# A one-core encoder layer in split fp32: layer norm by pairs of tiles, loads of the mixed rows deferred, the output weights in the common ring, head 0's operands in other memory, and two pieces of attention ordered behind feed-forward products

## The chip, the cores and the metric

The kernel runs on 1 core of one Trainium2 chip. The metric is the device time of one execution in microseconds (us), taken as the median of several runs; lower is better. The engines of the core are TensorE (PE in the profile, with its weight loads as PEld), VectorE (DVE), ScalarE (ACT), GpSimd (POOL) and SyncE (SP), which here only issues DMAs. Each engine takes its own instructions in a fixed order and waits at each for what that instruction needs.

## What is computed

One layer of a streaming encoder for 1024 new frames (the prompt) and 32 next frames of a running stream (the sample), width 1024, all in fp32. Cut to what matters:

```
mod = silu(c) @ w_ada + b_ada                      # six rows: sh1 sc1 g1 sh2 sc2 g2
h   = x * (1 + sc1) + sh1
p   = h @ w_in                                     # columns of three groups of heads
hm  = mLSTM(4 heads of p)        # matrix memory, chunk by chunk
hf  = FoX(8 heads of p)          # softmax(q k^T / 8 + F_t - F_s) v, causal
hg  = u * (tril(ws) @ layer_norm(v) + bs)          # spatial gate
mix = concat(hm, hf, hg) @ w_o
x   = layer_norm(ALPHA * x + (1 + g1) * mix, ln1_g, ln1_b)
h   = x * (1 + sc2) + sh2
y   = (silu(h @ w_gate) * (h @ w_up)) @ w_down     # inner width 2816
x   = layer_norm(ALPHA * x + (1 + g2) * y, ln2_g, ln2_b)
```

The outputs are both streams and the new state: keys, values, decays, matrix memory and its normalisers, gate values.

## The kernel before

Activations lie transposed: 128 features on the partitions, frames along the free axis, and eight such tiles (k = 0 to 7) make the width of 1024. The frames are split in group 0 (frames 0 to 511) and group 1 (512 to 1023 and the 32 of the sample). Every large product is made three times, since each operand is split in a high part that TensorE takes at full rate (float32r) and the rest: `gemm` issues hi by hi (L117), hi by lo (L118) and lo by hi (L119) for each k. So 24 matmuls make one 128-column block of an output, with 256 or 512 frames at a time. A weight block comes through `weights`: a load of 512 KB into a `raw` buffer on SP's queue (L85), a cast on ScalarE to the high part `whi` (L104), and a subtraction on VectorE to the low part `wlo` (L105). Raw buffers, high parts and low parts have three places each, the rings of the pool `wp`; a ring's place is used again when its last reader is done.

The program is emitted in the order of the code, and a scheduler then sets the order on each engine from the dependencies and its own time estimates. Code can bind it: `issue_after(x)` keeps what is emitted under it behind the instruction x.

The stages that the change touches run from about 300 to 470 us. First the input projection ends: a unit per block of columns, where `head_unit` makes head 7's queries and keys for the first 512 frames, L408 to L416, and stores what later stages need in DRAM (L89; `dqh` and `dql` are the high and low parts of all heads' queries and keys). The attention of head 7 over group 0 follows: scores (`fox_s`, L783 and L784), masked maximum (L786, L787), exponent (L792), scaling (L796, L800), transposes (`fox_t`, L819), products with the values (L827, L832). In between, ScalarE and VectorE split the mixed rows of group 0 into `tm_ah` and `tm_al` (`wo_mix`, L1007 and L1008), and projection units of the heads 2 to 4 for the second half of the frames run (`fm_unit`; the evacuation in `evac_qk` is L369 to L372 and sends keys out as `o_kT`).

Then the output projection of group 0 is made in two passes of 256 frames (`wo_range`): for each of eight blocks m a weight block, 24 matmuls, and `sublayer_end`, which on VectorE multiplies by the gate and adds the residual `wo_z` (L1074). The first block of a pass gives the pivot of the layer norm (`ln_pivot`; its ones-matmul is L932). Of the eight weight blocks six stay for the second pass. The first layer norm (`ln1`) works off a pass tile by tile, k = 0 to 7: times r (L1091), plus e (L1092), an ACTIVATE with scale and bias (L1095), a cast to the high part `tm_ah` (L1099), the subtraction for `tm_al` (L1100). The second pass is woven with the norm of the first, and the norm of the second with the projection units of the heads 5 to 7.

From about 443 us the feed-forward of group 0 runs: `up` makes a gate block and an up block per j (24 matmuls each, 256 frames at a time for j = 0, 512 from j = 1), `down` the way back. The attention over the frames 512 to 1023 (`mixers`: heads 0 to 7, chunks 4 and on of the mLSTM) is emitted ahead of it, to be taken in between its products until about 850 us. `fox` loads a head's operands from DRAM, first `qp`, then `k1` (`fox_k`), `q2`, `k2`, `v`, into tiles of the pool `mx1`. That pool lies where the pools `p1` and `sm` of the projection lay, and a load into it waits until the tiles that lay there are done. Modulation rows (`ada`, L179 to L193) are made in between too, with raw weights in the same ring.

## Time and profile before

| | |
|---|---|
| runs | 1363.7 us median of 3 (1363.5 to 1365.64) |
| profiled execution | 1364.8 us |
| its span from the first to the last instruction | 1362.7 us |
| instructions | 25189 |
| DMA packets | 120377, 221.70 MB |
| busy ACT, POOL of the span | 48%, 17% |

The profiled execution has its own time, which is 2.1 us over its span; the 2.1 us lie ahead of the first and behind the last instruction. In the timeline each row has a start and a duration in us, the engine, the line of the kernel, the operation, what it writes and reads, its shape, and in brackets how long the engine stood idle ahead of it and what ended that. Matmuls overlap: a row says 0.28 us for 128x256, but the next starts 0.12 us later.

### The profile page before, as it was taken

What the parts mean: (1) busy time and instruction counts of PE and PEld (TensorE: products, weight loads), DVE (VectorE), ACT (ScalarE), POOL (GpSimd) and SP (SyncE); (2) the same over time, 40 slices, a digit from 0 to 9 for tenths busy, and PEclk for the clock granted to TensorE, in tenths of its full rate; (3) what the DMA queues carried; (4) which work ended last, traced back from release to release, by engine and by line L of the source; (5) the groups of instructions that cost most, each with busy time, mean ns of one, the idle gap of its engine ahead of it and who ended that gap; (6) DMA issues with size and microseconds to landing.
All of it is one profiled execution on the core that took longest, in us unless ns stands there. A gap on an engine that the chain in (4) does not pass through costs nothing.

```text
span 1362.7 us, 25189 instructions
## 1 busy us (share of the span) xinstructions
PE 1327.6 (97%) x9434; PEld 1210.1 (89%) x9434; DVE 992.2 (73%) x2127; ACT 658.5 (48%) x1312; POOL 227.8 (17%) x263
## 2 busy tenths in 40 slices
PE   7999999998999899999999999999999999999996
PEld 4898988987999777888888888999999999999995
DVE  5545654678769667786776765678988988889777
ACT  3324454455436544545445354336663554545355
POOL 0202100043234200000000000373710000000341
PEclk9999999999999899999999999999999999999999
DMA  9775555546454765454344334574596758454321
GB/s 358 257 246 164 167 193 149 179 139 197 150 188 140 202 191 173 117 156 135 105 123 119 109 105 132 155 182 124 167 254 168 201 154 222 143 173 127 98 81 66
DMA packets 120377, 221.70 MB, mean 163 GB/s; under 512 B 18740, under 2 KB 64464, under 8 KB 120256
## 3 DMA queue, kind: packets, MB, share of 16 engines
q1 hardware_dynamic: 113024, 207.55, 48.7%
q0 software_dynamic: 6032, 11.94, 5.1%
q8 instruction: 74, 1.21, 0.4%
q10 hardware_dynamic: 1200, 0.62, 0.2%
q14 instruction: 47, 0.39, 0.1%
HBM read 188.13 MB, written 51.85 MB: 176 GB/s over the span
## 4 chain that ended last, share of the span: by engine, by line
PE 86%; DVE 6%; DMA 4%; ACT 2%; issue 1%; POOL 0%; SPq 0%; DVEq 0%; ACTq 0%
PE up_g L118 5%; PE up_g L119 5%; PE up_g L117 5%; PE dn_g L117 4%; PE dn_g L119 4%; PE dn_g L118 4%; PE tm_g L284 3%; PE tm_g L285 3%; PE tm_g L286 3%; PE sup_u L119 3%; PE sup_u L117 3%; PE sup_u L118 3%; PE fox_t L819 2%; PE fm_g L117 2%; PE sup_g L118 2%; PE sup_g L119 2%
## 5 line engine op out<-in xcount | busy, mean ns | idle before, releaser
L118 PE MATMUL up_g<-tm_al,up_whi 128*128 128x512 f32 (+1 forms) x384 | 141.3, 368 | 0.5 <-DVE tm_al L1100 0.5
L117 PE MATMUL up_g<-tm_ah,up_whi 128*128 128x512 f32 (+1 forms) x384 | 141.5, 370 | 0.2
L119 PE MATMUL up_g<-tm_ah,up_wlo 128*128 128x512 f32 (+1 forms) x384 | 140.6, 366 | 0.0
L1219 ACT CAST sup_whi<-sup_raw 128x1024 fp32r<-128x1024 f32 x54 | 56.0, 1048 | 90.9 <-PE dn_u L118 47.5
L117 PEld LDWEIGHTS up_g<-tm_ah,up_whi 128*128 128x128 f32 x384 | 72.8, 190 | 12.5 <-ACT tm_ah L1099 0.6
L118 PEld LDWEIGHTS up_g<-tm_al,up_whi 128*128 128x128 f32 x384 | 73.3, 191 | 11.0 <-DVE tm_al L1100 0.7
L119 PEld LDWEIGHTS up_g<-tm_ah,up_wlo 128*128 128x128 f32 x384 | 73.3, 191 | 10.7
L792 ACT ACTIVATE fox_p<-fox_s,fox_fmx 128x384 f32<-128x384 f32 (+2 forms) x96 | 55.1, 579 | 46.7 <-DVE fox_fmx L790 38.1
L104 ACT CAST up_whi<-up_raw 128x1024 fp32r<-128x1024 f32 x50 | 52.4, 1047 | 49.7 <-PE up_g L118 18.5
L1220 DVE TENSOR_TENSOR sup_wlo<-sup_raw,sup_whi 128x1024 fp32r<-128x1024 f32 x54 | 68.2, 1267 | 10.4 <-ACT sup_whi L1219 10.3
L1074 DVE SCALAR_TENSOR_TENSOR wo_z<-dn_g,start_mod,wo_z 128x512 f32<-128x512 f32 (+4 forms) x120 | 60.3, 521 | 20.1 <-PE dn_g L119 19.8
L105 DVE TENSOR_TENSOR up_wlo<-up_raw,up_whi 128x1024 fp32r<-128x1024 f32 x50 | 65.4, 1308 | 12.1 <-ACT up_whi L104 11.4
L117 PE MATMUL dn_g<-up_acth,dn_whi 128*128 128x512 f32 (+2 forms) x200 | 74.1, 371 | 0.0
L119 PE MATMUL dn_g<-up_acth,dn_wlo 128*128 128x512 f32 (+2 forms) x200 | 73.4, 367 | 0.0
L118 PE MATMUL dn_g<-up_actl,dn_whi 128*128 128x512 f32 (+2 forms) x200 | 72.9, 365 | 0.0
L824 ACT CAST fox_pth<-fox_t 128x512 fp32r<-128x512 f32 (+1 forms) x80 | 41.1, 545 | 55.9 <-PE fox_t L819 55.8
L104 ACT CAST dn_whi<-dn_raw 128x1024 fp32r<-128x1024 f32 (+1 forms) x44 | 42.7, 970 | 51.5 <-PE dn_u L118 11.2
L787 DVE TENSOR_REDUCE fox_fmx<-fox_s 128x1 f32<-128x384 f32 (+2 forms) x96 | 52.6, 552 | 13.5 <-PE fox_s L784 12.3
L825 DVE TENSOR_TENSOR fox_ptl<-fox_t,fox_pth 128x512 fp32r<-128x512 f32 (+1 forms) x80 | 49.4, 631 | 15.7 <-ACT fox_pth L824 15.5
L105 DVE TENSOR_TENSOR dn_wlo<-dn_raw,dn_whi 128x1024 fp32r<-128x1024 f32 (+1 forms) x44 | 49.5, 1126 | 12.6 <-ACT dn_whi L104 11.8
L284 PE MATMUL tm_g<-tm_whi,start_h1h 128*128 128x256 f32 (+1 forms) x192 | 55.9, 291 | 1.8 <-DVE tm_traw L355 1.7
L285 PE MATMUL tm_g<-tm_wlo,start_h1h 128*128 128x256 f32 (+1 forms) x192 | 56.1, 292 | 0.0
(663 smaller groups left out, 4788.9 us busy)
## 6 DMA issues: line engine op xcount, KB each, us to landing
up_raw<-w_gu SPq DMA_DIRECT2D x50, 512.0 KB
dn_raw<-w_dn SPq DMA_DIRECT2D x28, 512.0 KB
ada_late<-w_ada SPq DMA_DIRECT2D x24, 512.0 KB
sup_raw<-w_gu SPq DMA_DIRECT2D x20, 512.0 KB
start_dp<-w_gu SPq DMA_DIRECT2D x19, 512.0 KB
start_dp<-w_gu POOLq DMA_DIRECT2D x19, 512.0 KB, 8.0
wo_raw<-w_o SPq DMA_DIRECT2D x18, 512.0 KB
sup_raw<-start_dp SPq DMA_DIRECT2D x18, 512.0 KB
```

Source lines behind the costliest of these rows:

```text
L104: nc.scalar.copy(hi[:, :w], raw[:, :w])
L105: (eng or nc.vector).tensor_tensor(lo[:, :w], raw[:, :w], f(hi[:, :w]), ALU.subtract)
L117: nc.tensor.matmul(ps, hi, xh(k), start=start and k == 0, stop=False)
L118: nc.tensor.matmul(ps, hi, xl(k), start=False, stop=False)
L119: nc.tensor.matmul(ps, lo, xh(k), start=False, stop=stop and k == n - 1)
L284: nc.tensor.matmul(ps[:, :ncol], xh, hi, start=k == 0, stop=False)
L285: nc.tensor.matmul(ps[:, :ncol], xh, lo, start=False, stop=False)
L787: nc.vector.tensor_reduce(mxs[:, x:x + 1], s[:, :w], AX.X, ALU.max, negate=True)
L792: nc.scalar.activation(pr[:, lo:hi], banks[x][:, :hi - lo], AF.Exp, bias=mxs[:, 0:1], accum_out=sums[:, x:x + 1])
L1074: self.lastz = self.nc.vector.scalar_tensor_tensor(z[:, m, x:y], ps[:, x - a:y - a], g[i], z[:, m, x:y], ALU.mult, ALU.add)
L1219: nc.scalar.copy(h, x)
L1220: tt(l, x, f(h), ALU.subtract)
```

## The change

Five edits, all around the stages from 300 to 470 us:

1. **Pools.** The buffers of the evacuated queries and keys (`qkh`, `qkl`, `qkr`) move from the pool `sm` to a new pool `sq` between `p1` and `sm`; `wsp`, the spatial weights, moves from `p1` to `sm`. With that, the tiles of head 0 in `mx1` come to lie over other tiles.
2. **Mix loads.** The first six loads of mixed rows of group 0, with their casts and subtractions, are emitted under `issue_after` of head 7's last store of its operands.
3. **Common ring.** In the first pass of the output projection the weight blocks m = 3, 4, 5 lie in the pool `pw`, where m = 0, 1, 2 did, and these now take places of the ring in `wp`. The second pass runs over m = 2, 6, 7, 3, 4, 5, 0, 1 and loads 0 and 1 again (before: 0, 5, 6, 7, 3, 4, 1, 2, loading 3 and 4 again); the residual's second half comes in the order (2, 6), (4, 0), and the pivot is taken of the pass's first block.
4. **Norm by pairs.** For group 0 the layer norm takes two tiles per instruction on VectorE and in the cast. The ACTIVATE stays per tile, and each pair's multiplication is ordered behind the addition of the pair ahead of it.
5. **Ties.** The TensorE, ScalarE and VectorE instructions of head 0's first tile of scores are ordered behind the last matmul of the up block of j = 0, frames 256 to 511; the first two parts of mLSTM chunk 4 behind the last of the gate block of j = 1.

```diff
+    def traced(self, part):
+        n = len(self.nc.cur_bb.bb.instructions)
+        next(part)
+        return self.nc.cur_bb.bb.instructions[n:]
+    def tie(self, ins, target, engines):
+        for i in ins:
+            if i.engine in engines and "DMA" not in type(i).__name__ and "Dma" not in type(i).__name__:
+                self.tc.add_manual_dep(i, target.ins.name, ... reason="order")
...
-            hi = self.t(self.sm, [P, 272], F32R, "qkh", 2)
-            lo = self.t(self.sm, [P, 272], F32R, "qkl", 2)
-            kr = self.t(self.sm, [P, 272], F32, "qkr", 2)
+            hi = self.t(self.sq, [P, 272], F32R, "qkh", 2)
+            lo = self.t(self.sq, [P, 272], F32R, "qkl", 2)
+            kr = self.t(self.sq, [P, 272], F32, "qkr", 2)
...
-        self.store(self.dql[h, hi, :512], f(k2[lo]))
+        self.lastq = self.store(self.dql[h, hi, :512], f(k2[lo]))
...
-            w = kept.get(m) or self.weights(self.d["w_o"][m], KT, P, None, pool if m < 3 else None)
+            w = kept.get(m) or self.weights(self.d["w_o"][m], KT, P, None, pool if 3 <= m < 6 else None)
...
-                    for k in ((0, 4), (6, 2))[m // 7]:
+                    for k in ((2, 6), (4, 0))[m // 7]:
...
+        if c == 0:
+            yield from self.ln1_pairs(z, hh, hl, sl, r, e)
+            return
...
+    def ln1_pairs(self, z, hh, hl, sl, r, e):
+        nc, n = self.nc, sl.stop - sl.start
+        two = lambda x: x.unsqueeze(1).to_broadcast([P, 2, n])
+        last = None
+        for k in range(0, KT, 2):
+            yield
+            self.phase = "lna0"
+            zk = z[:, k:k + 2, sl]
+            with self.tc.issue_after(last.ins) if last else ExitStack():
+                nc.vector.tensor_tensor(zk, zk, two(r), ALU.mult)
+            last = nc.vector.tensor_tensor(zk, zk, two(e), ALU.add)
+            h = self.t(self.p2, [P, 544], F32, "sil", 2)[:, :2 * n].rearrange("p (k n) -> p k n", k=2)
+            for i in range(2):
+                nc.scalar.activation(h[:, i], zk[:, i], AF.Identity, bias=self.lnb[:, k + i, 0:1],
+                                     scale=self.lng[:, k + i, 0:1])
+            nc.scalar.copy(hh[:, k:k + 2, :n], h)
+            nc.vector.tensor_tensor(hl[:, k:k + 2, :n], h, f(hh[:, k:k + 2, :n]), ALU.subtract)
...
+                if c == 0 and (j, i) in ((0, 1), (1, 0)) and b == 512:
+                    eng = mybir.EngineType
+                    self.tie(self.tied[j], self.lastmm, (eng.PE, eng.Activation, eng.DVE))
...
+            if h == 0:
+                self.tied = [self.traced(parts[0])]
             if h in MLB:
-                parts.append(slow(self.mlstm(self.nextm)))
+                part = self.mlstm(self.nextm)
+                if h == 1:
+                    self.tied += [self.traced(part) + self.traced(part)]
+                parts.append(slow(part))
...
+        self.sq = self.pool("sq", 2, ctx=s1, side="right")
         self.sm = self.pool("sm", 2, ctx=s1, side="right")
...
-        self.wsp = self.t(self.p1, [P, 4, P], F32, "wsp")
+        self.wsp = self.t(self.sm, [P, 4, P], F32, "wsp", 1)
...
-        self.wo_mix(0, self.KORDER[0][:6])
+        with tc.issue_after(self.lastq.ins):
+            self.wo_mix(0, self.KORDER[0][:6])
...
-            del kept[3], kept[4]
-            weave(self.wo_range(st, *MM[0][1], (0, 5, 6, 7, 3, 4, 1, 2), kept, pw), self.ln1(0, st, *MM[0][0]))
+            del kept[0], kept[1]
+            weave(self.wo_range(st, *MM[0][1], (2, 6, 7, 3, 4, 5, 0, 1), kept, pw), self.ln1(0, st, *MM[0][0]))
```

How the change moves instructions is shown at three places, in the order in which the engine takes them. Numbers behind an underscore are buffer numbers, which count differently in the two programs, and the changed file's lines lie 11 to 35 further down. The first place is ScalarE around head 7's operands. `head_g` is the bank that holds them, `head_k` and `head_q` what the scores wait for, L1007 (L1018 after) the casts of the mixed rows. Before:

```order
L297 COPY tm_tmsum_4425<-tm_g_4416 64x256
L1007 CAST tm_ah_4595<-tm_al_4596 128x512 x2
L410 CAST head_k_755_4094<-head_g_4102 64x512
L1007 CAST tm_ah_4595<-tm_al_4596 128x512
L299 COPY tm_g_4416<-tm_tmsum_4425 32x256
L1007 CAST tm_ah_4595<-tm_al_4596 128x512 x2
L339 ACTIVATE mlstm_mrs_4206<-mlstm_mvar_4203,start_eps_39_119 128x4
L412 CAST head_k_755_4094<-head_g_4102 64x512
L413 ACTIVATE head_q_758_4097<-head_g_4102 64x512
```

With the change:

```order
L308 COPY tm_tmsum_4428<-tm_g_4419 64x256
L421 CAST head_k_755_4097<-head_g_4105 64x512
L310 COPY tm_g_4419<-tm_tmsum_4428 32x256
L350 ACTIVATE mlstm_mrs_4209<-mlstm_mvar_4206,start_eps_39_119 128x4
L351 ACTIVATE mlstm_mrs_4209<-mlstm_mrs_4209 128x4
L423 CAST head_k_755_4097<-head_g_4105 64x512
L424 ACTIVATE head_q_758_4100<-head_g_4105 64x512
```

Five casts of mixed rows stood between or just ahead of the two copies into `head_k`; none does now, and they come 5 to 20 rows later, between the exponents of head 7 (L792, now L803).

The second place is SP's queue at the loads of head 0's operands for the second attention, with the semaphores that each waits for (DMAHW and DMASW are earlier DMAs, DVE, PE, Activation and Pool the engines). Before:

```order
L85 DMA up_raw_7947<-w_gu 128x1024 [waits DMAHW5_49,DMAHW4_49,DVE_49]
L85 DMA fox_qp_5799<-start_dqh_57 64x512 [waits DMASW4_49,DMASW5_49,DMASW3_49,DMASW6_49,DMASW2_49,DMAHW0_49,DMASW1_49,DMAHW3_49,Activation_49,Pool_49]
L85 DMA fox_qp_5799<-start_dql_58 64x512 [waits DMAHW6_49]
L85 DMA fox_k_1018_5797<-start_dqh_57 64x1024 [waits DMAHW7_49,PE_49]
L85 DMA fox_k_1018_5797<-start_dqh_57 64x1024
```

With the change:

```order
L85 DMA up_raw_7911<-w_gu 128x1024 [waits DMAHW7_49,DMAHW6_49,DVE_49]
L85 DMA fox_qp_5763<-start_dqh_57 64x512
L85 DMA fox_qp_5763<-start_dql_58 64x512 [waits DMAHW0_49]
L85 DMA fox_k_1010_5761<-start_dqh_57 64x1024 [waits DMAHW1_49,PE_49]
L85 DMA fox_k_1010_5761<-start_dqh_57 64x1024 [waits DMAHW2_49]
L85 DMA fox_q_1013_5764<-start_dqh_57 64x512 [waits DMAHW3_49]
L85 DMA fox_q_1013_5764<-start_dfs_64 4x4x128 [waits DMAHW4_49]
L85 DMA fox_k_1011_5762<-start_dql_58 64x1024 [waits DMAHW5_49]
L85 DMA fox_k_1011_5762<-start_dfs_64 4x8x128 [waits DMAHW6_49]
L85 DMA fox_v_5765<-start_dv_59 128x8x128 [waits DMASW4_49,DMASW3_49,DMASW5_49,DMASW2_49,DMASW6_49,DMASW1_49,DMAHW7_49,Activation_49,Pool_49]
```

The long list of waits has gone from `fox_qp` to `fox_v`, four loads behind `fox_k`; `fox_qp` still stands behind the load of the up block of j = 1.

The third place is VectorE at the norm of the second pass, ahead of the feed-forward. Before:

```order
L970 SCALAR_TENSOR_TENSOR wo_pv_4860<-lna_tmp_5494,wo_pv_4860 128x256
L981 SCALAR_TENSOR_TENSOR wo_qs_4859<-lna_t_5490,wo_pv_4860 128x256
L1091 TENSOR_TENSOR wo_z_895_4846<-wo_z_895_4846,wo_pv_4860 128x256 x8
L1092 TENSOR_TENSOR wo_z_895_4846<-wo_z_895_4846,wo_qs_4859 128x256 x2
L370 SCALAR_TENSOR_TENSOR fm_qkl_5767<-fm_g_5741,start_qsc_147,fm_qkh_5766 128x272
L1092 TENSOR_TENSOR wo_z_895_4846<-wo_z_895_4846,wo_qs_4859 128x256 x3
L105 TENSOR_TENSOR up_wlo_7944<-up_raw_7941,up_whi_7943 128x1024
L1092 TENSOR_TENSOR wo_z_895_4846<-wo_z_895_4846,wo_qs_4859 128x256 x3
L1100 TENSOR_TENSOR tm_al_4596<-lna_tmp_5505,tm_ah_4595 128x256
```

With the change:

```order
L992 SCALAR_TENSOR_TENSOR wo_qs_4862<-lna_t_5473,wo_pv_4863 128x256
L1126 TENSOR_TENSOR wo_z_895_4849<-wo_z_895_4849,wo_pv_4863 128x2x256
L381 SCALAR_TENSOR_TENSOR fm_qkl_5655<-fm_g_5629,start_qsc_147,fm_qkh_5654 128x272
L1127 TENSOR_TENSOR wo_z_895_4849<-wo_z_895_4849,wo_qs_4862 128x2x256
L1126 TENSOR_TENSOR wo_z_895_4849<-wo_z_895_4849,wo_pv_4863 128x2x256
L116 TENSOR_TENSOR up_wlo_7763<-up_raw_7760,up_whi_7762 128x1024
L1127 TENSOR_TENSOR wo_z_895_4849<-wo_z_895_4849,wo_qs_4862 128x2x256
L1126 TENSOR_TENSOR wo_z_895_4849<-wo_z_895_4849,wo_pv_4863 128x2x256
L381 SCALAR_TENSOR_TENSOR fm_qkl_5696<-fm_g_5670,start_qsc_147,fm_qkh_5695 128x272
L1133 TENSOR_TENSOR tm_al_4599<-lna_sil_5488,tm_ah_4598 128x2x256
```

Before, all eight multiplications come first, then the additions, and the first low part (L1100) stands behind them. Now a pair is finished before the next begins, the first low part stands behind two and a half pairs, and when the norm begins, three evacuations of queries and keys (L370, now L381) are still to come instead of one.

23 lines of the change are left out of this document (13 added, 10 removed).

## The prediction, made before the changed kernel had run

> **What bounds the kernel now.** I read the page's first part, then TensorE's waits, then windows, then timelines of the places that stood out.
>
> ```profile
> PE 1327.6 (97%) x9434; PEld 1210.1 (89%) x9434; DVE 992.2 (73%) x2127; ACT 658.5 (48%) x1312; POOL 227.8 (17%) x263
> PE ada_t L179 <- DMA ada_araw<-w_ada: 7.2, 2, 5.9
> PE fox_s L783 <- DMA fox_k<-start_dqh: 3.8, 1, 3.8
> PE fox_s L783 <- ACT head_k L412: 3.0, 1, 3.0
> PE wo_t L932 <- DVE wo_z L1074: 1.7, 1, 1.7
> PE fox_t L819 <- DVE fox_p L800: 1.2, 2, 0.6
> ```
>
> The first row gives busy us, share of the span, instructions; the others what TensorE waited for: us in total, times, longest. TensorE is busy for 97%, so time is to be had only where it waits or runs slowly. The largest wait, on `ada_araw`, is at the start and nothing here touches it. Of the next, three sit in the changed stages: I call them C (3.8), A (3.0) and B (1.7). Windows, with busy us and count of PE, PEld, DVE, ACT, POOL, then the granted clock, show what the waits drag behind them:
>
> ```profile
> 330.00:335.60 5.60, 2.56 (x23) 2.10 (x22) 5.47 (x12) 5.06 (x12) 0.82 (x2) 1.00 0.96 361
> 335.60:339.00 3.40, 3.40 (x18) 3.40 (x17) 3.21 (x17) 1.38 (x6) 0.00 (x0) 0.50 0.54 162
> 382.00:386.00 4.00, 4.00 (x32) 3.95 (x33) 3.59 (x4) 1.70 (x3) 2.32 (x2) 1.00 0.94 235
> 443.00:449.00 6.00, 5.97 (x51) 5.76 (x49) 6.00 (x16) 4.31 (x10) 1.85 (x1) 1.00 0.43 154
> 455.20:459.20 4.00, 0.31 (x3) 0.11 (x1) 0.23 (x1) 0.00 (x0) 1.11 (x2) 0.91 0.94 229
> 459.20:465.30 6.10, 6.03 (x25) 5.84 (x26) 1.47 (x7) 1.84 (x3) 0.00 (x0) 0.50 1.11 222
> 466.00:545.00 79.00, 78.39 (x488) 62.29 (x487) 55.83 (x126) 40.12 (x91) 1.27 (x2) 1.00 0.63 191
> ```
>
> Behind A the clock is 0.50 for 3.4 us, behind C for 6.1 us, behind B it stays 1.00. At half clock a busy stretch does half its work, so the losses are 1.7 and 3.05 us on top of the waits. From 466 us on TensorE hardly ever stands still: what is won earlier is kept there unless something new is late.
>
> **The change part by part. A, the mix loads deferred.** Timelines of TensorE, ScalarE and VectorE (start, duration):
>
> ```profile
> 333.89 0.49 PE L783 MATMUL fox_s<-head_k,head_qp 128*128 128x128 f32 x2 [3.04 <-ACT head_k L412]
> 330.39 0.58 ACT L410 CAST head_k<-head_g 64x512 fp32r<-64x512 f32 x1 [0.54 <-DVE head_qp L409]
> 330.99 0.62 ACT L1007 CAST tm_ah<-tm_al 128x512 fp32r<-128x512 f32 x1
> 331.64 0.37 ACT L299 COPY tm_g<-tm_tmsum 32x256 f32<-32x256 f32 x1
> 332.03 1.14 ACT L1007 CAST tm_ah<-tm_al 128x512 fp32r<-128x512 f32 x2
> 333.07 0.29 ACT L339 ACTIVATE mlstm_mrs<-mlstm_mvar,start_eps 128x4 f32<-128x4 f32 x1
> 333.27 0.57 ACT L412 CAST head_k<-head_g 64x512 fp32r<-64x512 f32 x1
> 330.72 0.40 DVE L298 TENSOR_TENSOR tm_tmsum<-tm_g,tm_tmsum 64x256 f32<-64x256 f32 x1
> 331.05 1.27 DVE L1008 TENSOR_TENSOR tm_al<-tm_al,tm_ah 128x512 fp32r<-128x512 f32 x2
> ```
>
> The scores wait for L412, and ahead of it stand three casts of mixed rows. L410 ends at 330.97 as before, since L409 ahead of it is untouched. Without the casts L299 follows when L298 is done (331.12): to 331.5; L339's input is no longer behind L1008's 1.27 us, so it runs to 331.8; L340, as small (0.3), to 332.1; L412 to 332.7. That is 1.2 us earlier than 333.84 (between 0, if the rest of VectorE's row is late, and 2.3, if L412 follows L410 at once). The wait is then 1.8 us, nearly B's; behind B the clock stayed full, behind 3.0 us it fell. So I count the 1.7 us of half clock as gone: A gives 2.9.
>
> The Trainium skill (TensorE: Matmul & The Clock Gate, "Part 1: The HAM clock gate") says that the gate looks at a free-running window of about 3.4 us, so that where a gap falls in it counts as well. The trace agrees in the length, 3.4 us at 0.50 behind A; that a wait under 3.4 us tripped it at all fits the running window. By that rule a wait of 1.8 us could still be unlucky, and the sum would be 1.7 us higher; that lies within the range below.
>
> The five deferred casts (0.57 us each by the row of two, 2.9 us together) and as many subtractions (0.64, 3.2 us) land between head 7's exponents. There is room:
>
> ```profile
> 340.61 0.30 DVE L786 TENSOR_TENSOR fox_s<-fox_s,start_maskneg 128x128 f32<-128x128 f32 x1 [1.75 <-PE fox_s L784]
> ```
>
> VectorE idles there, ScalarE is busy for 1.38 of the 3.40 us of the window behind A, and TensorE has projection products ahead of the transposes. One cast stands ahead of an exponent; I take 0.3 us lost, between 0 and 1.8 (three casts at once ahead of the last exponent).
>
> **B, the common ring.** The pivot's matmul waits for L1074, queued on VectorE behind L105:
>
> ```profile
> 381.99 0.70 PE L932 MATMUL wo_t<-wo_z,start_ones 128*128 128x256 f32 x2 [1.73 <-DVE wo_z L1074]
> 380.32 1.23 DVE L105 TENSOR_TENSOR wo_wlo<-wo_raw,wo_whi 128x1024 fp32r<-128x1024 f32 x1 [6.00 <-ACT wo_whi L104]
> 381.46 0.48 DVE L1074 SCALAR_TENSOR_TENSOR wo_z<-wo_g,start_mod,wo_z 128x256 f32<-128x256 f32 x1
> 379.24 1.05 ACT L104 CAST wo_whi<-wo_raw 128x1024 fp32r<-128x1024 f32 x1 [5.98 <-DMA wo_raw<-w_o]
> ```
>
> VectorE had idled 6.0 us in front of a subtraction whose weights were late, with the pivot's operation behind it. Now the weight block ahead of L1074 is one whose load stands ahead of the residual loads on SP, and the late ones follow behind L1074. Then the pivot is ready under the second product: the whole 1.7 us goes; if the load is late again, none. I take 1.5. What comes next, the weights of m = 4 and 5, is needed three and four products (24 x 0.118 = 2.8 us each) later, and casts behind them are hidden so.
>
> **C, pools, pairs and ties.** TensorE waits for `fox_k`, with SP's queue ahead of it:
>
> ```profile
> 459.27 0.90 PE L783 MATMUL fox_s<-fox_k,fox_qp 128*128 128x384 f32 x2 [3.76 <-DMA fox_k<-start_dqh]
> 448.53 0.33 SPq L85 DMA_DIRECT2D up_raw<-w_gu  x1
> 452.64 0.48 SPq L85 DMA_DIRECT2D fox_qp<-start_dqh  x1
> 454.56 1.17 SPq L85 DMA_DIRECT2D fox_k<-start_dqh  x2
> SPq L85 <- DMA o_kT<-fm_qkr: 3.1, 1, 3.1
> 442.52 2.76 DVE L1091 TENSOR_TENSOR wo_z<-wo_z,wo_pv 128x256 f32<-128x256 f32 x8
> 449.42 0.82 DVE L1100 TENSOR_TENSOR tm_al<-lna_tmp,tm_ah 128x256 fp32r<-128x256 f32 x2
> 449.90 0.39 PE L118 MATMUL up_g<-tm_al,up_whi 128*128 128x256 f32 x1 [0.49 <-DVE tm_al L1100]
> ```
>
> The `fox_qp` load waited 3.1 us for the last store of keys, because it lands where that store's buffer lies. In the new order it waits for nothing of its own and follows the `up_raw` load, 0.5 us behind it: 449.0 instead of 452.6, so `fox_k` is issued at 450.9 and, at the 4.7 us from its first issue to the scores, is there at 455.6. TensorE, which came to the scores at 455.5 (459.27 - 3.76), now has all 96 of the 256-frame matmuls of j = 0 ahead of them instead of 80, at 0.118 us (6.00 us for 51) 1.9 more, fewer of the modulation, and loses less ahead of them (below): it comes at 455.6 or a little later. So of the 3.8 us 0.2 stay, and with the rest goes the 3.05 us of half clock. Moreover the `up_raw` load itself waits for a subtraction that stood behind the norm; being earlier, it may pull the loads forward by up to 1 us.
>
> The norm: L1091's eight took 2.76 us, and the first low part came 6.9 us behind their start. By pairs (a 128x2x256 operation lies between one and two of the 0.35 us above; I take 0.7) the first low part stands behind five such operations and an evacuation, about 4 us, and the norm starts two evacuations earlier. TensorE needs the second half of the frames only 48 matmuls (5.7 us) into the feed-forward. The 0.5 us of wait goes, and some 0.4 us (an estimate) of matmuls that follow the low parts one by one: 0.9. Fewer VectorE and ScalarE instructions elsewhere lie under TensorE and give nothing. C: 3.6 + 3.05 + 0.9 = 7.5, between 0.9 (the loads no earlier) and 8.
>
> **What could be late next** is the feed-forward's weights, since TensorE comes 11.6 us earlier to them (rows of the chain of waits):
>
> ```profile
> 476.45 3.79 DMA up_raw<-w_gu
> 480.26 1.06 ACT up_whi L104
> 481.34 1.23 DVE up_wlo L105
> 467.05 0.24 PE up_g L117
> ```
>
> One raw buffer is loaded, cast, subtracted and loaded again: 3.79 + 1.06 + 1.23 = 6.1 us a block, while TensorE takes 24 x 0.24 = 5.8 us for it and what attention puts between. The chain is as long in the new order, but its first load takes another place of the ring, freed by the modulation's products instead of by the subtraction of the block before it. I take 1 us lost, between 0 and 5 (0.5 us for each of ten blocks).
>
> **Sum.** 2.9 - 0.3 + 1.5 + 7.5 - 1.0 = 10.6 us. The profiled execution took 1364.8 us, 1.1 above the median of 1363.7; against the median: 1353.
>
> **The rivals.** *fox_k still late.* `fox_qp` stands behind `up_raw`, 512 KB that share the DMA engines (0.94 busy at 455 to 459), and that load waits for VectorE. If `fox_k` lands 3 us after TensorE arrives, the half clock stays too: C gives 1.5, and the time is 1359. For it: the row of 0.94; against it: the queue is freed 3.6 us earlier.
>
> *The weights take it back.* If the ring is the bound from 466 us on, each block costs its 6.1 us, and the 5 us above go: 1357. For it: the chain runs through it; against it: 78.39 of 79 us busy.
>
> *Attention becomes the wait, slower.* The ties and the new order leave fewer products between a tile's scores and its transposes in heads 0 and 1:
>
> ```profile
> 475.31 1.14 ACT fox_p L792 x3
> ```
>
> In the chain a tile's exponents took 1.14 us; with the maximum ahead and the scaling behind I estimate twice that and a little, 2.5 us. Of 16 groups of tiles (8 heads, two each), if six or more stand uncovered for 2.5 us, 15 us go and the kernel is slower, at 1368; below four it stays faster. For it: already TensorE waits for L800 (1.2 us, two times). Against it: that is all over the whole kernel, and from head 2 on the order has at least as many products in between.
>
> *It doesn't do what it says*: all three waits are only moved to the next load or evacuation, within 2.7 us of before.
>
> **How the numbers follow.** The sum 0.53; fox_k late 0.17; weights 0.11; waits only moved 0.07; attention slower 0.12. Predicted is the likeliest, 1353. Its own range is 1349 (A at 4.0, C at 8, nothing lost) to 1356; the range goes on to both middle rivals and a little more: 1349 to 1363. A measurement of this kernel tells 0.2% (2.7 us) from no change: faster 0.81, same 0.07, slower 0.12.
>
> **What would show it.** Right, if TensorE's wait for head 7's scores is below 2 us with the clock at 1.00 behind it, its wait for the pivot is gone, and its wait for `fox_k` is under 1 us with no half clock around 450 to 460; and if the feed-forward from there to its end takes as long as before. Wrong, if a wait of over 3 us stands ahead of head 0's scores, if `up_raw` or `fox_p` appears among TensorE's waits, or if the stretch up to 850 us has grown.

## The result, and the profile after

The changed kernel takes 1361.21 us in the median of 20 runs (1356.46 to 1365.73), the kernel before 1365.62 (1362.4 to 1369.06, 20 runs beside them). The ratio is 0.9969, with a 95% interval of 0.9959 to 0.9979: 4.4 us faster, between 2.9 and 5.6. The direction was right; of the 10.6 us forecast less than half came. The profiled execution took 1363.44 us, 2.2 above its median, so single stages are compared here, not spans.

The first part of the page after, and TensorE's waits after (those of the changed stages), in the columns known from the prediction:

```profile
PE 1328.2 (98%) x9434; PEld 1207.9 (89%) x9434; DVE 994.9 (73%) x2103; ACT 659.6 (48%) x1304; POOL 233.2 (17%) x263
```

```profile
PE wo_g L128 <- ACT tm_ah L1018: 2.4, 2, 2.1
...
PE tm_g L735 <- DVE tm_tmsum L311: 1.6, 1, 1.6
...
PE up_g L128 <- DVE up_sil L1186: 0.8, 1, 0.8
...
PE up_g L130 <- DVE up_wlo L116: 0.5, 1, 0.5
...
PE up_g L128 <- ACT up_whi L115: 0.4, 1, 0.4
PE fox_s L794 <- DMA fox_k<-start_dqh: 0.4, 1, 0.4
```

All three waits of the prediction are gone or small: head 7's scores wait for nothing (1.6 us is left, of the spatial gate's products ahead of them, L735), the pivot's wait has no row, `fox_k` costs 0.4 instead of 3.8. But the largest row is new: the output projection waits 2.4 us for the mixed rows' casts, `tm_ah`. Windows of the changed kernel around those places (busy us and count of PE, PEld, DVE, ACT, POOL, then granted clock, DMA share, GB/s):

```profile
333.60:338.40 4.80, 4.60 (x39) 4.18 (x39) 3.51 (x15) 3.24 (x10) 0.00 (x0) 1.00 0.81 245
379.00:385.00 6.00, 5.85 (x28) 5.58 (x28) 3.61 (x5) 3.01 (x4) 1.53 (x3) 0.52 1.07 394
443.00:466.00 23.00, 21.87 (x160) 19.19 (x160) 15.10 (x26) 13.34 (x28) 10.09 (x10) 1.00 0.86 202
466.00:545.00 79.00, 78.09 (x490) 61.30 (x489) 57.96 (x135) 40.80 (x91) 1.37 (x3) 1.00 0.64 189
```

Behind A (334 to 338) and around C (443 to 466) the clock is full. The half clock now stands at 379 to 385, around and behind the new wait, in the stage where B was to gain.

To place the gain I cut the program, in each profile, at TensorE rows that all versions have. In the changed kernel these are:

```profile
326.20 1.07 PE L306 MATMUL tm_g<-tm_raw,start_hs 128*32 128x256 f32 x16
...
372.76 0.28 PE L128 MATMUL wo_g<-tm_ah,wo_whi 128*128 128x256 f32 x1
...
426.36 0.30 PE L130 MATMUL wo_g<-tm_ah,wo_wlo 128*128 128x256 f32 x1
...
445.47 0.28 PE L128 MATMUL up_g<-tm_ah,up_whi 128*128 128x256 f32 x1
...
874.07 0.29 PE L128 MATMUL wo_g<-up_ah,wo_whi 128*128 128x272 f32 x1
```

Stretch A runs from the last matmul of the first row's block (at 326.90) to the first `wo_g`, B from there to the last `wo_g` of group 0, C from the first `up_g` to the first `wo_g` of the second group. The 19 us between B and C and the time ahead of A and behind C hardly change (19.5 before and 19.1 with the change, but 28.2 in e14; 325 to 328; 474.5 to 475.5 to TensorE's last matmul). In brackets stands what half clock cost in the stretch at most: the sum over windows of 1 us of length times (1 - granted clock). It comes in steps of 1.7 us, that is stretches of 3.4 us at 0.50. Where half clock sets in while TensorE still waits, that part costs nothing: of the 3.4 us in C before, some 0.5, since 458.2 to 459.3 us lie in the wait for `fox_k`. Each row is one profile; medians are of 5 to 20 timed runs, and each ratio is taken against runs of the kernel before made beside them.

| kernel | A | B | C | A to C | median us | ratio, 95% interval |
|---|---|---|---|---|---|---|
| before | 48.72 (1.7) | 49.20 (0) | 433.04 (3.4) | 550.45 | 1365.62 | 1 |
| before, again (e15) | 50.42 (3.4) | 48.70 (0) | 431.60 (1.7) | 550.21 | | |
| changed | 45.86 (0) | 53.60 (3.4) | 428.60 (0) | 547.17 | 1361.21 | 0.9969, 0.9959 to 0.9979 |
| changed, again (e8) | 47.48 (1.7) | 51.21 (1.7) | 429.21 (0) | 547.01 | 1360.83 | 0.9963, 0.9951 to 0.9975 |
| e1 without deferred mix loads | 48.89 (3.4) | 50.69 (0) | 429.58 (0) | 548.26 | 1364.46 | 0.9993, 0.9978 to 1.0008 |
| e2 without common ring | 46.62 (1.7) | 49.13 (0) | 430.39 (0) | 545.20 | 1362.85 | 0.9985, 0.9969 to 1.0 |
| e3 without the pools | 45.85 (0) | 53.50 (3.4) | 430.88 (0) | 549.33 | 1362.59 | 0.9987, 0.9969 to 1.0006 |
| e4 without pairs | 45.61 (0) | 51.72 (1.7) | 434.49 (1.7) | 550.98 | 1367.01 | 1.0013, 0.9993 to 1.0032 |
| e6 without ties | 47.02 (1.7) | 50.93 (1.7) | 428.74 (0) | 545.80 | 1362.14 | 0.9968, 0.9957 to 0.998 |
| e7 pairs alone | 49.97 (3.4) | 48.40 (0) | 435.06 (0) | 552.49 | 1365.69 | 1.0003, 0.999 to 1.0016 |
| e11 deferred mix loads alone | 46.72 (1.7) | 48.75 (0) | 432.71 (3.4) | 547.66 | 1363.49 | 0.9991, 0.9977 to 1.0006 |
| e12 common ring alone | 49.29 (1.7) | 49.22 (0) | 435.16 (1.7) | 552.81 | 1368.40 | 1.0019, 1.0003 to 1.0034 |
| e5 fourth weight load later | 45.41 (0) | 49.82 (0) | 431.62 (1.7) | 545.96 | 1360.81 | 0.9965, 0.9952 to 0.9977 |
| e9 that, and modulation later | 46.93 (1.7) | 48.26 (0) | 432.26 (0) | 546.56 | 1363.39 | 0.9986, 0.9973 to 0.9999 |
| e10 modulation later | 46.94 (1.7) | 48.76 (0) | 432.49 (0) | 547.30 | 1364.93 | 0.9998, 0.9982 to 1.0014 |
| e13 e5, late loads on GpSimd | 45.84 (0) | 48.61 (0) | 433.54 (0) | 547.09 | 1363.93 | 0.9986, 0.9975 to 0.9996 |
| e14 e5, modulation spread | 46.96 (1.7) | 48.77 (0) | 432.74 (6.9) | 556.62 | 1373.03 | 1.0054, 1.0038 to 1.0069 |
| e16 e5, modulation cut | 47.06 (1.7) | 48.33 (0) | 430.49 (0) | 544.98 | 1363.01 | 0.9976, 0.9962 to 0.9989 |

By the means of the two profiles of each, A gains 2.9 us, C 3.4 and the piece between 0.4, and B loses 3.5: 3.2 us net, against 4.4 in the medians. Half clock costs 5.1 us over the three stretches in both profiles of before and 3.4 in both of the changed kernel. One profile more or less moves a stretch by 1 to 2 us, and mostly it is this lottery; so means over several profiles, and the stretches without their brackets, carry more than a single cell. Without the brackets A gains 1.2 us, C 0.8 and the piece between 0.4, and B loses 0.9: of the 3.2 us net, 1.7 are half clock and 1.5 the rest.

### The profile page after: what moved, and what is told of

Its sections match the earlier page's. It is cut to its first block, busy times and chain, and to the rows that moved or that the text cites. A ratio compares the mean times of both kernels' runs of the same rounds, so it can differ in the third digit from the quotient of the medians.

```text
span 1360.6 us, 25153 instructions
## 1 busy us (share of the span) xinstructions
PE 1328.2 (98%) x9434; PEld 1207.9 (89%) x9434; DVE 994.9 (73%) x2103; ACT 659.6 (48%) x1304; POOL 233.2 (17%) x263
## 4 chain that ended last, share of the span: by engine, by line
PE 87%; DVE 5%; DMA 4%; ACT 2%; issue 1%; SPq 1%; DVEq 0%; ACTq 0%
PE up_g L130 6%; PE up_g L128 6%; PE up_g L129 6%; PE dn_g L128 4%; PE dn_g L130 4%; PE dn_g L129 4%; PE tm_g L295 3%; PE tm_g L297 3%; PE tm_g L296 3%; PE sup_u L130 3%; PE sup_u L128 3%; PE sup_u L129 3%; PE wo_g L129 2%; PE fox_t L830 2%; PE wo_g L130 2%; PE wo_g L128 2%
## 5 line engine op out<-in xcount | busy, mean ns | idle before, releaser
L115 ACT CAST up_whi<-up_raw 128x1024 fp32r<-128x1024 f32 x50 | 52.5, 1049 | 68.3 <-PE up_g L129 26.1
L129 PEld LDWEIGHTS up_g<-tm_al,up_whi 128*128 128x128 f32 x384 | 72.2, 188 | 10.6
L803 ACT ACTIVATE fox_p<-fox_s,fox_fmx 128x384 f32<-128x384 f32 (+2 forms) x96 | 55.1, 578 | 37.5 <-DVE fox_fmx L801 29.4
L116 DVE TENSOR_TENSOR dn_wlo<-dn_raw,dn_whi 128x1024 fp32r<-128x1024 f32 (+1 forms) x44 | 49.5, 1126 | 12.9 <-ACT dn_whi L115 12.2
```

Of the source, the lines that this page charges most:

```text
L115: nc.scalar.copy(hi[:, :w], raw[:, :w])
L116: (eng or nc.vector).tensor_tensor(lo[:, :w], raw[:, :w], f(hi[:, :w]), ALU.subtract)
L129: nc.tensor.matmul(ps, hi, xl(k), start=False, stop=False)
L803: nc.scalar.activation(pr[:, lo:hi], banks[x][:, :hi - lo], AF.Exp, bias=mxs[:, 0:1], accum_out=sums[:, x:x + 1])
```

## The experiments

**One edit undone (e1 to e4, e6) and the changed kernel again (e8).** The edits, in the numbering of the section on the change:

```diff
e1 (edit 2 undone)
-        with tc.issue_after(self.lastq.ins):
-            self.wo_mix(0, self.KORDER[0][:6])
+        self.wo_mix(0, self.KORDER[0][:6])
e2 (edit 3 undone)
-            w = ... self.weights(..., pool if 3 <= m < 6 else None)
+            w = ... self.weights(..., pool if m < 3 else None)
-                    for k in ((2, 6), (4, 0))[m // 7]:
+                    for k in ((0, 4), (6, 2))[m // 7]:
-            del kept[0], kept[1]
+            del kept[3], kept[4]
-            weave(self.wo_range(..., (2, 6, 7, 3, 4, 5, 0, 1), ...
+            weave(self.wo_range(..., (0, 5, 6, 7, 3, 4, 1, 2), ...
e3 (edit 1 undone)
-            hi = self.t(self.sq, [P, 272], F32R, "qkh", 2)
+            hi = self.t(self.sm, [P, 272], F32R, "qkh", 2)
...
-        self.wsp = self.t(self.sm, [P, 4, P], F32, "wsp", 1)
+        self.wsp = self.t(self.p1, [P, 4, P], F32, "wsp")
e4 (edit 4 undone)
-        if c == 0:
-            yield from self.ln1_pairs(z, hh, hl, sl, r, e)
-            return
e6 (edit 5 undone)
-                if c == 0 and (j, i) in ((0, 1), (1, 0)) and b == 512:
+                if False:
```

> The changed kernel with edit 2 undone: the mix loads are no longer ordered behind head 7's stores, edits 1, 3, 4, 5 stay. Theory 1 (deferring the mixed rows pushes the last mLSTM chunk's transposes 18 rows back on TensorE, so the last two mixed rows reach the output projection late): TensorE's wait for head 7's scores is back at about 3 us with half clock behind it (+2.9 us), the wait of the first output product for tm_ah (2.4 us in the changed kernel) and the half clock behind it are gone (-4.8 us), and the pivot is ready under the second product: about 1359 us. Theory 2 (the common ring's early fourth weight load shares the DMA engines with the mixed rows): the wait for tm_ah stays at 2 us or more beside A's: 1363 to 1364 us. Theory 3 (one slow DMA engine by chance): no wait for tm_ah, in this kernel nor in the next.

> The changed kernel with edit 3 undone: weight blocks 0 to 2 in the separate pool, second pass 0, 5, 6, 7, 3, 4, 1, 2. Theory 1: the wait for tm_ah stays, somewhat smaller since the transposes stand 11 instead of 18 rows later (1 to 2 us), and the pivot waits as before: 1359 to 1363 us. Theory 2: the wait for tm_ah is gone, with the half clock: about 1357 us.

> The changed kernel with edit 1 undone: the buffers of queries and keys and the spatial weights lie in the pools of before. If the earlier loads of head 0's operands came from the pools, TensorE waits 2 to 4 us for fox_k again with half clock behind it, and the time is 4 to 7 us longer than the changed kernel's 1361.2: 1365 to 1368 us. If the ties alone brought it, the wait stays under 1 us and the time at 1361 us.

> The changed kernel with edit 4 undone: the first layer norm of group 0 tile by tile. If the pairs only took 0.9 us of waits for the low parts, TensorE waits for tm_al again, 0.5 to 1 us, and the time is 1361.5 to 1362.5 us. If the pairs also freed the second half's operands and SP's queue, fox_k is late by 2 us or more, with half clock: 1364 to 1367 us.

> The changed kernel with edit 5 undone: no ties. If the ties matter, the scores of head 0 stand among the first products again, TensorE waits 1 us or more for fox_k, and the stretch from the first feed-forward product to the second output projection is 430 to 432 us instead of 428.6: 1363 to 1365 us. If the loads come early enough without, under 0.5 us of wait and 1361 us.

> The changed kernel once more, for the spread between profiles: 1361 us; if the wait for tm_ah is a matter of the kernel it is there again at 1.5 to 3 us with a store of 3.5 us or more ahead of it, if it was one slow DMA engine by chance it is gone and the profiled run is about 1357 us.

Measured: the table. *e1*: A takes 48.89 us again, but not for the reason forecast. Its wait for head 7's scores is half of the 3.0 us expected:

```profile
PE fox_s L794 <- ACT head_k L423: 1.5, 1, 1.5
```

The rest is half clock, one step behind this wait and one behind an earlier wait of 1.9 us (L366); without its bracket A is 45.5, as in the changed kernel. B loses the wait for `tm_ah`, as theory 1 has it, but takes 50.69, since waits of 2.7 us for `wo_z` (VectorE's residual sums) come in its place, and the time is 1364.46, not 1359. *e2*: with the ring as before, the pivot waits 1.7 us again, but the wait for `tm_ah` and the half clock behind it are gone, so B falls to 49.13: what the ring gains at the pivot it more than loses at the mixed rows. The time of 1357 that theory 2 gave did not come (1362.85), since C takes 1.5 us more than in the changed kernel, with a new wait of 1.2 us for `start_qks`. *e3*: `fox_k` waits 1.8 us (0.4 with the edit) and C takes 2 us more than the changed kernel's 428.9, so the pools count, but much less than I had put on them (one profile; 1362.59 us, where 1365 to 1368 was expected). *e4*: without the pairs C takes 434.49, 5.6 us more (1.7 of it half clock), and the whole gain is gone (1367.01, the upper end of what was expected). *e6*: C 428.74, no wait for `fox_k`, the time 0.9968: the ties gain nothing that shows. *e8*: the spread of one order; the same wait for `tm_ah` shows (1.7 us) with half as much half clock behind it.

**One edit alone (e7, e11, e12).** The kernel before, with edit 4, 2 or 3 only.

> The kernel before with edit 4 alone: the norm of group 0 by pairs, nothing else. Theory P (the pairs free SP's weight load and the last evacuation, and so carry most of what the changed kernel wins at fox_k): the loads of fox_qp are issued 7 us or less behind the first feed-forward product instead of 9.5, the wait for fox_k is under 1.5 us, and the time 1360 to 1362 us. Theory Q (the pools or the ties carry it): fox_qp at 9 us or later, the wait of 3 to 4 us with half clock stays, 1364 to 1366 us.

> The kernel before with edit 2 alone. The stretch to the first output product is 46 us instead of 48.7 (the wait for head 7's scores near 1.6 us, no half clock), the 16 output products take 49 to 50 us with the pivot's wait as before, the rest as before: 1362.5 to 1363.5 us. If the deferral alone makes the mixed rows late, the 16 products take over 51 us and the time is 1365 us.

> The kernel before with edit 3 alone. If the ring is what makes the norm of the second half early (first low part 3 to 4 us behind the first feed-forward product instead of 6.3) but costs time in the output products (50 to 51 us instead of 49.2), the wait for fox_k shrinks to 1 to 3 us and the time is 1363 to 1366 us; the pivot's wait is gone, but waits of output products for wo_z, 1 to 3 us, stand in its place.

Deferring alone takes A to 46.72 and leaves B (48.75), as forecast; the time is 0.1% lower, which its interval (0.9977 to 1.0006) does not tell from no change. The ring alone removes the pivot's wait and puts 1.5 us for `wo_z` in its place, as its forecast had it, so that B stays (49.22); at 1368.40 it is slower than forecast. Pairs alone and the ring alone make C slower, 435.06 and 435.16 where before has 432.3 on average: in the one the products wait 1.6 us for `start_qks` and 1.7 for `up_whi` (and only 0.8 for `fox_k`, since TensorE comes to it later), in the other 1.1 for `fm_qkr` and 0.9 for a low part. With all five edits it is 429. So C's gain is of no one edit: pairs and ring pay only in company, and which of the small waits decides that is not settled.

**Where B's loss comes from (e5).** The theory after e1 and e2: the last two of the eight mixed rows, chunks of the mLSTM, are late for two reasons at once. First, deferring the loads moves the last chunk's transposes nearer to the output projection. Rows of TensorE's timeline, before and after:

```profile
365.05 0.38 PE L700 MATMUL mlstm_t<-start_ident,mlstm_mhm 128*128 128x128 f32 x2
...
374.45 0.28 PE L117 MATMUL wo_g<-tm_ah,wo_whi 128*128 128x256 f32 x1
```

```profile
365.74 0.38 PE L711 MATMUL mlstm_t<-start_ident,mlstm_mhm 128*128 128x128 f32 x2
...
372.76 0.28 PE L128 MATMUL wo_g<-tm_ah,wo_whi 128*128 128x256 f32 x1
```

From the second transpose (0.1 us behind the row's start) to the first `wo_g` there are 9.3 us before and 6.9 after. (With the deferral it is 6.9 in eleven profiles and 7.8 in e2 and e11; without it 9.3 in all.) Second, the ring puts a fourth weight load on SP just ahead of the store of that chunk. SP's queue, before and after:

```profile
366.47 0.37 SPq L89 DMA_DIRECT2D start_dmix<-mlstm_mtot  x1
...
368.32 0.80 SPq L85 DMA_DIRECT2D tm_al<-start_dmix  x2
...
371.27 0.41 SPq L85 DMA_DIRECT2D wo_raw<-w_o  x1
```

```profile
363.27 0.39 SPq L85 DMA_DIRECT2D wo_raw<-w_o  x1
...
367.86 0.37 SPq L89 DMA_DIRECT2D start_dmix<-mlstm_mtot  x1
371.66 0.32 SPq L85 DMA_DIRECT2D tm_al<-start_dmix  x1
...
372.50 0.42 SPq L85 DMA_DIRECT2D tm_al<-start_dmix  x1
```

Before, `wo_raw` follows the two loads; after, it is issued 4.6 us ahead of the store, and the store takes 3.8 us to release its load instead of 1.85. The chain of waits of the changed kernel runs through just these, and through the mixed row ahead of them (start, duration, what):

```profile
362.86 4.06 DMA tm_al<-start_dmix
...
367.46 0.37 ACT mlstm_mtot L713
...
367.86 3.78 DMA start_dmix<-mlstm_mtot
...
372.50 5.50 DMA tm_al<-start_dmix
378.00 0.02 issue
378.03 0.63 ACT tm_ah L1018
378.65 0.02 issue
378.68 0.70 DVE tm_al L1019
379.38 0.04 issue
379.42 0.58 PE wo_g L129
```

From the transposes to the last subtraction it takes 13.5 us (8.7 before), and the products need it 9.3 us behind them (6.9 + some 2.4 for the six rows ahead). The fourth weight load meets this way twice. It follows the load of the row ahead by 0.4 us; that load takes 4.1 us (2.8 in e5 below, where the weight load is not there), and its cast stands on ScalarE ahead of the copy `mlstm_mtot` that the store sends out, so the store is issued 2.0 us behind the transposes. Then the store itself is slow. The test holds back that load alone, behind the last mix load:

```diff
-                self.load(f(l), self.dmix[0][:, k])
+                self.mixload = self.load(f(l), self.dmix[0][:, k])
...
-            w = kept.get(m) or self.weights(...)
+            with self.tc.issue_after(self.mixload.ins) if a == 0 and m == 3 else ExitStack():
+                w = kept.get(m) or self.weights(...)
```

> The changed kernel with one load moved: the fourth weight block of the output projection (m = 3) is ordered behind the last load of mixed rows; SP's queue alone changes there. Theory A (that load, 3 to 5 us ahead of the mLSTM's store, doubles the store's time, 3.8 to 4.4 us against 1.8, and the deferral has already taken 2.4 us of the lead): the store is back at about 1.9 us, the last low part comes 11 us behind the transposes instead of 12.8 to 14, the wait for tm_ah shrinks from 1.6 to 2.9 us to under 1 us without half clock, the stretch of the 16 output products is 50 us instead of 51.7 to 53.6, and the time 1358 us. Theory B (the deferral alone makes the mixed rows late): the wait stays over 1.5 us and the time at 1361 us.

SP's queue in e5, and two windows of it in B:

```profile
366.22 0.37 SPq L89 DMA_DIRECT2D start_dmix<-mlstm_mtot  x1
368.66 0.32 SPq L85 DMA_DIRECT2D tm_al<-start_dmix  x1
...
369.50 1.31 SPq L85 DMA_DIRECT2D tm_al<-start_dmix  x1
...
373.43 0.49 SPq L85 DMA_DIRECT2D wo_raw<-w_o  x1
```

```profile
374.90:380.00 5.10, 4.60 (x35) 4.18 (x34) 2.72 (x4) 1.61 (x3) 1.54 (x3) 1.00 1.00 338
380.00:386.00 6.00, 5.57 (x46) 5.21 (x44) 3.75 (x5) 2.79 (x5) 2.24 (x2) 1.00 1.01 355
```

The load is released after 2.4 us, there is no half clock, and B takes 49.82 us. The other four versions that hold that load back (e9, e13, e14, e16) take 48.26 to 48.77 there; the six with both edits and without the hold take 48.76 to 53.60, 51.6 on average. That this load, together with the deferral, costs B its loss is shown. How it does so is shown in part: with the hold the store is issued 0.75 us behind the transposes instead of 2.0 and takes 1.4 us less, and the last low part comes 10.4 us behind them instead of 13.5. But in e8 and e10 the store takes only 2.35 and 2.28 us without the hold, no more than the 2.2 to 2.4 of the versions with it; there the late issue (1.7 and 1.9 us) and the load behind it remain, the last low part comes 12.0 and 11.1 us behind, and in e10 the wait is 0.9 us and B 48.76. The kernel is no faster for the hold: 1360.81 against 1361.21 and 1360.83 us. What B won, C lost: 2.7 us, 1.7 of them half clock.

**Where it is given back (e9, e10).** The waits of e5, and its chain, at the weights of the gate block of j = 2:

```profile
PE up_g L128 <- ACT up_whi L115: 1.7, 1, 1.7
...
PE up_g L130 <- DVE up_wlo L116: 0.5, 1, 0.5
```

```profile
463.90 7.33 DMA up_raw<-w_gu
...
471.25 1.05 ACT up_whi L115
...
472.32 1.24 DVE up_wlo L116
...
473.61 0.80 PE up_g L130
```

e5 reaches the feed-forward 4 us earlier than the changed kernel (441.3, 445.5), but these weights land only 2.5 us earlier (471.25, 473.79). Two loads of modulation weights, 512 KB each, are issued right ahead of them. e9 (with e5's edit) and e10 (without) move the modulation:

```diff
-                if j < 4:
-                    self.ada(20 + j, ...)
+                for u in {2: (20, 21), 3: (22, 23)}.get(j, ()):
+                    self.ada(u, ...)
```

> The kernel with the fourth weight load later, and with the loads and products of the modulation rows 20 to 23 emitted behind the up blocks of j = 2 and 3 instead of j = 0 to 3. Theory W (after the output projection the next limit is the load of the gate weights of j = 2, which stands on SP behind 18 small loads and two of 512 KB for the modulation and takes 7 us among them): those weights come ahead of head 0's operands, TensorE's waits for up_whi and up_wlo at 472 to 476 us (1.7 + 0.5, with half clock behind) are gone, the stretch from the first feed-forward product to the second output projection is 3 to 4 us shorter than 431.6, and the time 1357 to 1358 us. Rival (the modulation's loads only collide with the next blocks): the waits return at j = 3 or at the first way back, 1360 to 1362 us.

> The changed kernel with only the modulation rows moved as in the run before. Theory W: the wait for tm_ah stays (1.5 to 3 us), the waits for up_whi (0.4 to 1.2 us) go: 1359 to 1360 us. Rival: 1361 us or more.

The waits at j = 2 go, and come back at j = 3 and at the first down product; C is 432.26 and 432.49, the times 1363.39 and 1364.93 us (0.9986 and 0.9998), no better than without and above what either theory gave. Moving the loads moves the wait.

**Queue or bandwidth (e13, e14, e16).** Is it SP, with 18 loads of the attention and the mLSTM to issue ahead of the modulation and those weights, or are the DMA engines full? (e15 is the kernel before once more: its B, 48.70, lies in the range expected, its C, 431.60, 0.9 us below it.) e13 is e5 with the mLSTM loads of chunks 4 on issued by GpSimd; e14 is e5 with two modulation rows ahead of the feed-forward and two spread behind it; e16 is e5 with a quarter of the modulation rows' bytes; it leaves out three quarters of those weights, so its output is another.

```diff
e13
+        ld = self.load if j < 4 else lambda out, in_: nc.gpsimd.dma_start(out, in_)
-        self.load(qk[:, :, :L], self.dmqk[:, :, o:o + L])
+        ld(qk[:, :, :L], self.dmqk[:, :, o:o + L])
...
e14
+        for u in (20, 21):
+            self.ada(u, ...)
...
-                if j < 4:
-                    self.ada(20 + j, ...)
+                for u in {0: (22,), 2: (23,)}.get(j, ()):
+                    self.ada(u, ...)
e16
+            if u >= 20:
+                nc.gpsimd.memset(raw[:, 256:], 0.0)
-            self.load(raw, self.d["w_ada"][u, :, half * 1024:(half + 1) * 1024])
+            self.load(raw[:, :n], self.d["w_ada"][u, :, half * 1024:half * 1024 + n])
```

> The changed kernel with the fourth weight load held back behind the mix loads, and with the mLSTM loads of the last chunks (which SP issues ahead of the gate weights of the second half's j=2) on GpSimd's DMA queue instead. Theory (what the change gains is given back behind the output projection because SP has 18 loads to issue ahead of the j=2 gate weights, 446.4 to 463.9 us without this edit): the j=2 gate weights are issued 3 us or more earlier, the waits for up_whi and up_wlo at 472 to 475 us (1.72 and 0.53) go, the stretch from the first feed-forward product to the second output projection falls from 431.6 to 429 us or less, and the time is near 1358 us, ratio 0.994 to 0.996. Rival (the DMA engines' bandwidth holds the weights, whoever issues them): the weights land as late, the waits stay within 0.5 us, the stretch stays at 430 to 433 and the time at 1360 to 1362, ratio 0.996 to 0.998.

> The changed kernel with the fourth weight load held back, and with the four modulation rows loaded elsewhere: two ahead of the feed-forward, one behind its first and one behind its fourth weight tile. Theory (SP's queue ahead of the j=2 weights): two to three loads fewer stand ahead of them, the waits at 472 to 475 us fall from 2.2 us in sum to under 1, and do not come back at j=3; time 1358 to 1360 us, ratio 0.994 to 0.996. Rival (the weights' own flow through the DMA engines is the bound of this stretch, so a wait taken from j=2 turns up at j=3 or at the down products): the waits in sum stay at 1.5 us or more, time 1360.5 to 1363, ratio 0.9965 to 0.9985.

> The kernel before once more, for the spread of its stretches between profiles. If the sign of the output projection's loss is real, its 16 products take 48.4 to 49.5 us here again (49.20 in the first profile), with no wait for tm_ah; if the first profile was a lucky one, 50.5 us or more. The stretch from the first feed-forward product to the second output projection should be 432.5 to 435 us (433.04 in the first).

> The changed kernel with the fourth weight load held back, and of each half of the four modulation rows of the feed-forward only the first quarter loaded (0.8 of 1.05 MB a row less, the rest of the buffer set to zero by GpSimd; the output is not the reference's, since three quarters of these modulation weights are left out). SP issues as many loads in the same order. Theory (the DMA engines' bandwidth holds the j=2 gate weights, which landed 28 to 30 us after the first feed-forward product in every run, also where they were issued 6 us earlier): with two quarter loads instead of two whole ones ahead of them they land 3 us or more earlier, at 27 us or less; the waits for up_whi and up_wlo there go, the stretch from the first feed-forward product to the second output projection falls from 431.6 to 428.5 or less, and the time is near 1358 us, ratio 0.993 to 0.9955. Rival (something else in the chain, the issues on SP or the buffers of the ring): they land at 28.5 us or later, the waits stay, 1360 to 1362, ratio 0.996 to 0.998.

The load in question on SP, in e5 and in e13 (the duration of a pair is that of both with the wait between them), and the cast that ends its way in e13:

```profile
462.76 1.04 SPq L85 DMA_DIRECT2D ada_raw<-w_ada  x2
463.90 0.38 SPq L85 DMA_DIRECT2D up_raw<-w_gu  x1
```

```profile
454.79 1.10 SPq L85 DMA_DIRECT2D ada_raw<-w_ada  x2
455.98 16.16 SPq L85 DMA_DIRECT2D up_raw<-w_gu  x2
```

```profile
469.48 1.04 ACT L115 CAST up_whi<-up_raw 128x1024 fp32r<-128x1024 f32 x1 [4.45 <-DMA up_raw<-w_gu]
```

From the first `up_g` (441.31 and 439.40) the weights are issued 22.6 us on in e5 and 16.6 in e13, and their cast starts 29.9 and 30.1 us on. Six us earlier in the queue gain nothing: the same 512 KB take 7.3 us in the one and 13.5 in the other. Windows of e13 and of e16 at that place show why:

```profile
450.00:465.00 15.00, 13.71 (x85) 11.11 (x84) 6.32 (x17) 8.36 (x21) 4.13 (x7) 1.00 1.05 229
```

```profile
450.00:465.00 15.00, 14.64 (x85) 11.60 (x86) 6.38 (x18) 6.14 (x18) 1.47 (x2) 1.00 1.06 228
```

The DMA share is above 1 for 15 us. It is the engines' time that runs out and not a rate of bytes: they move 229 and 228 GB/s here, and 394 at a share of 1.07 in the window at 379 us shown above. The Trainium skill (DMA: Bandwidth & Descriptors, "Issuing engines are not separate DMA queues") has it that loads from SP and GpSimd share the same DMA engines, so that another issuer saves issue time and no bandwidth. e13 agrees: issued 6.0 us earlier, the weights are there no earlier, and at 1363.93 us it is slower than either of its theories gave. e14 shows the other side: rows taken ahead stop TensorE right before the feed-forward (3.8 us for `ada_raw`), the weights wait all the same (5.1 us for `up_whi`, 3.7 of it at j = 1), and at 1373.03 us, outside both ranges, it is 0.5% slower.

e16 takes bytes away instead, and there the weights land 26.1 us behind the first `up_g`, earlier than in any profile that loads them in this order (27 to 33), and the wait for `up_whi` is gone. So what else the DMA engines have to move sets the landing (one profile), and not the place in SP's queue. But the expectation of C at 428.5 fails: 430.49, with 1.1 us of wait for `up_sil` (VectorE's products of the block ahead) at 470.5, where the weights had been late, and 2.5 us of waits in the attention at 494 to 506. The wait for `up_sil` is not free of the weights either. In this order VectorE has their subtraction ahead of those products, and stood idle for them:

```profile
467.96 1.22 DVE L116 TENSOR_TENSOR up_wlo<-up_raw,up_whi 128x1024 fp32r<-128x1024 f32 x1 [3.24 <-ACT up_whi L115]
```

The time, 1363.01, does not improve on e5 either.

## Why the prediction was wrong

The profiles gain 3.2 us of the 10.6 forecast. Of the 7.4 that are missing, 5.0 are B's and 3.1 C's; A and the piece between B and C came out 0.3 and 0.4 better. (The sum adds up; of its own range the lower end does not: with A at 4.0, B at 1.7 and C at 8 it is 1350, not 1349.)

**A held.** Over thirteen profiles with the deferral A takes 46.5 us, over five without 49.5: 3.0 gained, 2.6 forecast (2.9 less 0.3). But not quite in the way that was told. Without the half clock it is 45.4 against 46.7, so 1.3 us of wait, as computed (1.2); e1 alone, at 45.5 without the deferral, does not fit. The half clock fell from 2.7 to 1.05 us on average, not to nothing: the wait of 1.6 us left at L735 is the same in all thirteen, and in eight of them half clock follows, in five not. "I count the 1.7 us of half clock as gone" was too much for any single run. The changed kernel itself shows it both ways (first its window at 333.60 above, at 1.00; here e8's):

```profile
334.50:337.90 3.40, 3.37 (x17) 3.37 (x18) 2.71 (x12) 2.32 (x7) 0.00 (x0) 0.58 0.90 261
```

The Trainium skill's free-running window (TensorE: Matmul & The Clock Gate, "Part 1: The HAM clock gate"), quoted in the prediction as a chance of being unlucky, fits this better than a threshold between 1.7 and 3.0 us.

**B is the step that failed.** "Then the pivot is ready under the second product: the whole 1.7 us goes ... I take 1.5." The pivot's wait did go. B still lost 3.5 us, 5 us off, the largest error of the sum. Nor was the 1.5 us there without the collision: the five versions that hold the load back take 48.8 us on average against 49.0 before, with small new waits of 0.3 to 1.7 us (`tm_al`, `wo_qs`, `wo_wlo`) where the pivot's was. The step asked which weights come next and found them hidden; it did not ask what the moved load is moved past. In the new order the fourth weight load stands ahead of the mLSTM chunk's store and its two loads on SP, and A's own edit had just taken 2.4 us off those rows' lead (1.5 without the ring's order, e2 and e11). Neither edit alone costs B anything (e11 48.75, e12 49.22); together they make a wait of 1.6 to 2.9 us in five of six profiles, with 1.7 to 3.4 us of half clock around it (0.9 and none in the sixth, e10). The part on A priced the deferred casts among the exponents and not the transposes that changed places with them on TensorE.

**C was over-sized.** Forecast were 7.5 less 1.0 for late weights; 3.4 came (428.9 against 432.3), 2.6 of them half clock and only 0.8 of the rest. The pieces that were to go did go: `fox_k` 3.76 to 0.36 us, the norm's 0.5, the half clock. Three things were wrong with the sum. The half clock of 3.05 us was taken from one profile, where it cost two steps; in the second profile of before the same wait, 3.9 us, cost one, 1.7. New small waits came in: 0.8 for `up_sil`, 0.9 to 1.7 for the weights of j = 2, the term "late weights", which was right in kind and size. And the modulation's 64 products, which took 4.0 us from start to start before, take 6.0 and 6.5, of which 0.7 and 1.3 are waits; the first and the last of their four groups of 16 are now split (4 and 12, 10 and 6). The sum had nothing for that.

What was credited to what was also off. The gain was put on the pools, with the pairs at 0.9; e3 and e4 say that the pools are worth 2 us and the pairs, given the ring, 5.6. The forecast of `fox_k` came out: 12.5 us behind the first `up_g` by the sum (455.6), 13.4 measured, 16.1 and 16.2 before, and within 0.4 us of TensorE's coming.

**Half clock as a whole** carried 4.75 of the forecast 10.6 us. It fell from 5.1 to 3.4: not removed, but set behind another wait.

**The rivals.** "The weights take it back" is the one that the chip bears out, with two corrections: it is the time of the DMA engines and not one buffer's chain of load, cast and subtraction, and it holds only for some 15 us and not for ten blocks; from the first down product on, TensorE works without a wait to the second output projection, 361.7 us before and 362.7 after (some of the attention's products have moved behind that point). "fox_k still late" fell. "Attention becomes the wait" fell as well: `fox_p` among TensorE's waits takes 1.1 us, as before. That the waits are "only moved" is right for B and A together, not for the sum.

**What stays open:** why pairs and ring each make C slower alone, and the last microsecond between the profiles' 3.2 us and the medians' 4.4, which is within what one profile of each kernel varies by. No version found beats the changed kernel beyond its interval; e5 equals it.

## What to carry to other kernels

When a load is moved, list what it is moved past on its queue and on the DMA engines, and how much lead those have: two edits that each leave a margin can use it up together, so price them together. A half clock behind a wait is not a fixed term: take it as a chance over several profiles, and ask which wait will stand last once this one is gone. Where the DMA share is near 1 for longer than the wait that is to be won, an earlier place in a queue won nothing here (e13); less for the engines to move did bring the weights earlier (e16), though not the kernel's end.
